# One core, two layers and a mixer in fp32: longer chains of seven-product tile pairs in the MLPs

## The chip, the cores and the metric

The kernel runs on 1 core of one Trainium2 chip. The metric is the device time of one execution in microseconds. PE is the matmul engine, PEld its weight load, DVE the vector engine, ACT the scalar engine, POOL the GpSimd engine, SP the engine whose queue issues the weight loads.

## The reference, cut to what matters

Three blocks run one after the other on 512 tokens (the first two with 16 more in front) of width 1024: a differential attention layer with its MLP, a latent attention layer with its MLP, and a mixer block (convolution and windowed attention, gated) with a third MLP; a final norm ends it. The change touches only the three MLPs, which all have this form:

```python
def conv_ffn(h, g_norm, w_in, conv_w, conv_b, w_out):
    xn = rms_norm(h, g_norm)
    a, b = jnp.split(xn @ w_in, 2, axis=-1)        # 1024 -> 2 x 2816
    ap = jnp.pad(a, ((0, 0), (CONV_W - 1, 0), (0, 0)))
    a_conv = conv_b
    for j in range(CONV_W):
        a_conv = a_conv + ap[:, j:j + L] * conv_w[j]
    return h + (jax.nn.silu(a_conv) * b) @ w_out   # 2816 -> 1024
```

## The kernel before

**Numbers.** Everything is fp32, computed on the matmul engine in three passes: an operand is split into a high part (a cast) and a low part (operand minus high part), and a product is Xh·whi + Xl·whi + Xh·wlo. So every weight that is loaded is cast once by ACT (line 162, `whi`) and subtracted once by DVE (line 170, `wlo`) or, for some chunks ("far"), by POOL (line 112).

**Tile pairs.** w_in has 22 tile pairs of 128 gate columns (a) and 128 value columns (b). A pair is computed in one of two ways. `Plain` takes two weight chunks of 512 KB and makes 96 matmuls: 2 chunks x 2 column ranges x 8 k-tiles x 3 passes, printed as line 329. `Seven` treats the pair as a 2 x 2 by 2 x 2 block product (two halves of k, two column ranges) and makes it with seven block products instead of eight, 12 matmuls each, 84 in all, printed as line 553. `p1, p6, p7, p4` accumulate one after the other in one PSUM bank A, `p5, p3` in a second, C, and `p2` has its own; between them ACT copies a running sum out of the bank (u1 after p1, bm after p5, u2 after p6, bm after p4) and DVE adds one to a product (am after p2, bm after p7, am after p3). A product that goes on in bank A has to wait for the copy or the add that reads the bank. The differences of the input columns that the seven need are made once per MLP (`differences`).

**Weights of a seven.** Its two chunks (raw_0, and raw_1 in the two buffers of tag `rawA`) are loaded together. `combine` (line 129) has POOL make four sums of 128x512, two instructions of 128x256 each: rawS, then raw_1's low half, raw_0's low half and raw_0's high half, in place. Four split chunks come of them: "a" (raw_0 as loaded, for p1 and p2), "s" (rawS and raw_0's low half, for p5 and p6), "t" (raw_1's low half and raw_0's high half, for p7 and p3), "d" (raw_1's high half, for p4; its low part is made by POOL). The buffers of the split "s" and "d" are single: the next "d" can be cast only when p4 with the last one has ended.

**Order of the work.** `plan_ffn` lists the chunks in the order of use. `get` (lines 180 to 190) issues the splits two chunks ahead of the one asked for and the loads three ahead; loads go through one queue, SP's. A load of raw_1 waits until its buffer is free, that is until POOL's split of the "d" two sevens earlier has read it. PE's order inside `turns` is as written (`in_order`); the scheduler orders the other engines, and each runs its own list in order. The 22 pairs go in four groups; after each, `group_h` multiplies the group's gated tiles by their rows of w_out (printed `po`, line 329) and adds to h. 12 of the 22 pairs are `Seven`, in twos or singly with a plain pair between their products, and 10 are `Plain`.

Of the kernel before, what the change touches and what calls it, by code (L numbers as in the profile page):

```python
# [21 lines left out]
P = 128  # L22
# [5 lines left out]
NF = 22  # L28
# [12 lines left out]
def _layout_params():  # L41
# [14 lines left out]

NPAR = _layout_params()

GROUPS = (
    (0, 6, (0, 1, 2, (3, 4, 5))),  # L60
    (6, 11, ((6, 7, 8), (9, 10))),
    (11, 17, ((11, 12, 13), (14, 15, 16))),
    (17, 22, ((17, 18, 19), (20, 21))),
)

WSPEC = [
# [13 lines left out]
class Weights:  # L80
# [8 lines left out]
    def __init__(self, net, plan, gains, raw, parts, load_ahead, split_ahead):  # L89
        self.net, self.plan, self.gains = net, plan, gains  # L90
        self.raw, self.parts = raw, parts
        self.la, self.sa = load_ahead, split_ahead
        self.nl = self.ns = self.nu = 0
        self.raws, self.split = {}, {}
        self.more, self.rows = None, []

    def load(self):
        key, aps, nk, nc_, kind = self.plan[self.nl]
# [12 lines left out]
            c = slice(c, min(c + 256, w))  # L111
            self.net.nc.gpsimd.tensor_tensor(d[:, c], a[:, c], b[:, c], op=op)  # L112

    def sources(self, n, kind, w):

        lo, hi = slice(0, 512), slice(512, 1024)
        raws = self.raws.pop(n)
        if kind == "":
            return [raws[0][:, :w]]
        if kind == "a":  # L120
            self.rows.append(raws)
            return [raws[0]]
        a = self.rows[0]
        if kind == "s":
            return [a[2], a[0][:, lo]]
        if kind == "t":
            return [a[1][:, lo], a[0][:, hi]]
        return [self.rows.pop(0)[1][:, hi]]

    def combine(self):  # L130

        lo, hi = slice(0, 512), slice(512, 1024)
        a = self.rows[-1]
        d = self.more.tile([P, 512], F32, tag="rawS", name=f"rawS{self.ns}")
        a.append(d)
        self.sums(d, a[1][:, lo], a[1][:, hi], ALU.add)
        self.sums(a[1][:, lo], a[0][:, lo], a[1][:, lo], ALU.subtract)
        self.sums(a[0][:, lo], d, a[0][:, lo], ALU.subtract)
        self.sums(a[0][:, hi], a[0][:, hi], a[0][:, lo], ALU.subtract)

    def _split(self):
        nc = self.net.nc
        n = self.ns
        key, aps, nk, nc_, kind = self.plan[n]
        w = nk * nc_
        src = self.sources(n, kind, w)
        own = kind in ("s", "d")
        pool, tag, kw = (self.more, f"w{kind}", {"bufs": 1}) if own else (self.parts, "w", {})
        wide = 512 if kind == "d" else 1024
        hi = pool.tile([P, wide], F32R, tag=tag + "hi", name=f"whi{n}", **kw)  # L150
        lo = pool.tile([P, wide], F32R, tag=tag + "lo", name=f"wlo{n}", **kw)
        h, l = hi[:, :w], lo[:, :w]
        if key[0] in self.gains:
            for k in range(nk):
                c = slice(k * nc_, (k + 1) * nc_)
                self.net.split(h[:, c], l[:, c], src[0][:, c], self.net.pc(self.gains[key[0]], k))
        else:
            far = kind == "d" or kind == "" and (n % 4 == 3 or key[0] in ("w_pair", "w_qr"))
            c0 = 0
            for r in src:  # L160
                z = r.shape[-1]
                nc.scalar.copy(h[:, c0 : c0 + z], r)  # L162
                step = z if far else (z + 1) // (1 + (z > 512))
                for a in range(0, z, step):
                    b = min(a + step, z)
                    c = slice(c0 + a, c0 + b)
                    if far:
                        self.sums(l[:, c], r[:, a:b], h[:, c].bitcast(F32), ALU.subtract)
                    else:
                        nc.vector.tensor_tensor(l[:, c], r[:, a:b], h[:, c].bitcast(F32), op=ALU.subtract)  # L170
                c0 += z
            if kind == "a":
                self.combine()
        self.split[n] = (
            h.rearrange("p (k c) -> p k c", k=nk),
            l.rearrange("p (k c) -> p k c", k=nk),
        )
        self.ns += 1
# [27 lines left out]
class Net:  # L206
# [59 lines left out]

    def plan_ffn(self, wi, wo):
        pl = []
        for k0, k1, steps in GROUPS:
            for st in steps:  # L270
                if isinstance(st, int):
                    pl += [self.chunk(wi, st), self.chunk(wi, NF + st)]
                    continue
                *fs, g = st
                a, d = [[self.chunk(wi, m + f)[1] for f in fs] for m in (0, NF)]
                u = [
                    [((wi, f, "a"), a[i] + d[i], 8, P, "a"), ((wi, f, "s"), [], 8, P, "s")]
                    + [((wi, f, "t"), [], 8, P, "t"), ((wi, f, "d"), [], 4, P, "d")]
                    for i, f in enumerate(fs)
                ]  # L280
                wa, wb = self.chunk(wi, g), self.chunk(wi, NF + g)
                if len(u) == 1:
                    pl += [*u[0][:2], wa, u[0][2], wb, u[0][3]]
                else:
                    pl += [*u[0][:2], wa, u[0][2], u[1][0], u[0][3], u[1][1], wb, *u[1][2:]]
            pl += [self.chunk(wo, m, k0, k1) for m in range(KD)]
        return pl

# [206 lines left out]
    def ffn(self, wi, wo, cw, cb, a_ranges, b_ranges, quads, ranges, nxt, gain=None):  # L495
# [8 lines left out]
        n, o = NT - t0, t0 - a0  # L504
        (s0, e0), (s1, e1) = quads
        H = e0 - s0
        with ExitStack() as cx:
# [1 line left out]
            psp = cx.enter_context(tc.tile_pool(name=self.n("pf"), bufs=6, space=PSUM, reuse_waits="tile"))  # L509
            tp = xcx.enter_context(tc.tile_pool(name=self.n("ft"), bufs=2, reuse_waits="tile"))  # L510
            R, _ = self.norm(psp, "mm", int(a0 == META))
            kmax = max(k1 - k0 for k0, k1, _ in GROUPS)
# [90 lines left out]
            class Seven:  # L603
# [6 lines left out]
                lo, hi, sl = slice(0, H), slice(e0 - a0, NT - a0), slice(e0 - s1, H)  # L610
# [48 lines left out]
                    nc.vector.tensor_tensor(me.t, me.b[:, o : o + n], me.t, op=ALU.mult)  # L659
                    self.split(*G.at(me.k, t0, NT), me.t)  # L660

            def turns(k0, *fs):

                u = [Seven(f, f - k0) for f in fs[:-1]]
                v = Plain(fs[-1], fs[-1] - k0)
                x, y = u[0], u[-1]
                x.p1(), x.p5(), v.a(0), x.p6(), x.p2(), v.a(1), x.p7()
                if x is y:
                    v.b(0), x.p3(), x.p4(), v.b(1)
                    return  # L670
                x.p3(), y.p1(), x.p4(), y.p5(), y.p6(), y.p2(), v.b(0), y.p7(), y.p3(), v.b(1), y.p4()

            def add(p, m, s, e):
                nc.vector.tensor_tensor(self.h[:, m, s:e], p, self.h[:, m, s:e], op=ALU.add)  # L674

            for k0, k1, steps in GROUPS:
                for i, st in enumerate(steps):
                    if isinstance(st, int):
                        v = Plain(st, st - k0)
                        v.a(0, 2), v.b(0, 2)  # L680
                    else:
                        with self.in_order():
                            turns(k0, *st)
                    if k0 == i == 0:
                        differences()
                if k1 < NF:
                    self.group_h(psp, wo, G, k0, k1 - k0, ranges, add)
            xcx.close()
# [1210 lines left out]
```

## Time and profile before

| | |
|---|---|
| median of 3 runs | 2097.27 us (2091.37 to 2097.52) |
| profiled execution | 2097.7 us, span 2095.9 us, mean granted clock 0.992 |
| busy share | PE 98%, PEld 90%, DVE 67%, ACT 47%, POOL 35% |
| seven pairs, plain pairs per MLP | 12, 10 |
| the third MLP in the chain of waits | 1731 to 2085 us, PE throughout |

The span runs from the first to the last instruction of the profiled execution. A busy PE says that it always had a matmul to work on, and not how fast it could be; the other engines work beside it, and matter where PE has to wait for what they make.

### The profile page before, as it was taken

Reading aid. Unit: us, or ns where it says so; the run is one execution under the profiler, and the core shown is the slowest. Engines: PE = TensorE matmul, PEld = TensorE weight load, DVE = VectorE, ACT = ScalarE, POOL = GpSimd, SP = SyncE. Lnnn points to the kernel's source line nnn. Section 1 sums busy time; section 2 is a strip of 40 time slices with the busy share of each in tenths; the row PEclk is TensorE's granted clock in tenths of the full one; section 3 lists DMA queues with packets and bytes.
Section 4 is the critical chain, followed back from the end, with each engine's and each line's share of the span. In section 5 each row is a group of like instructions: output and inputs, shape, how many; then the busy total and the mean of one; then the engine's idle time right before and its main releaser. Section 6 shows DMA issues by size and latency. Waiting matters only on the chain. (4 is left out here: it accounts for less than half of the span.)

```text
span 2095.9 us, 36290 instructions
## 1 busy us (share of the span) xinstructions
PE 2047.9 (98%) x14327; PEld 1894.5 (90%) x14327; DVE 1398.0 (67%) x2536; ACT 976.9 (47%) x1940; POOL 738.6 (35%) x837
## 2 busy tenths in 40 slices
PE   8999999999999999999999999999999999999998
PEld 7999899999999988899898998788888879899997
DVE  8787768576767576658576768675533358577674
ACT  6566545253445455445344445354432235354444
POOL 5223252344343231133345444321112244435442
PEclk9999999999999999999999999999999999999999
DMA  4121132323322211022323333222223332323322
GB/s 169 52 61 55 38 106 67 101 80 103 102 83 82 67 41 41 32 91 66 112 82 95 94 100 92 93 81 77 70 76 101 96 116 64 108 85 108 105 76 72
DMA packets 56426, 174.91 MB, mean 83 GB/s; under 512 B 6464, under 2 KB 9408, under 8 KB 56256
## 3 DMA queue, kind: packets, MB, share of 16 engines
q1 hardware_dynamic: 55824, 172.34, 26.2%
q8 instruction: 112, 1.84, 0.4%
q14 instruction: 58, 0.48, 0.1%
q10 hardware_dynamic: 432, 0.27, 0.0%
HBM read 170.45 MB, written 2.10 MB: 82 GB/s over the span
## 5 line engine op out<-in xcount | busy, mean ns | idle before, releaser
L162 ACT CAST whi<-raw 128x1024 fp32r<-128x1024 f32 (+4 forms) x460 | 382.4, 840 | 555.3 <-PE po L329 176.8
L112 POOL TENSOR_TENSOR wlo<-raw,whi 128x256 fp32r<-128x256 f32 (+1 forms) x336 | 292.1, 897 | 582.7 <-ACT whi L162 564.7
L170 DVE TENSOR_TENSOR wlo<-raw,whi 128x512 fp32r<-128x512 f32 (+2 forms) x580 | 402.8, 732 | 44.3 <-ACT whi L162 41.4
L329 PE MATMUL pf<-Xh,whi 128*128 128x256 f32 (+2 forms) x960 | 273.0, 285 | 0.0
L329 PE MATMUL pf<-Xl,whi 128*128 128x256 f32 (+2 forms) x960 | 272.4, 284 | 0.0
L329 PE MATMUL pf<-Xh,wlo 128*128 128x256 f32 (+2 forms) x960 | 272.3, 284 | 0.0
L329 PE MATMUL po<-Gl,whi 128*128 128x512 f32 (+2 forms) x709 | 238.8, 338 | 0.0
L329 PE MATMUL po<-Gh,wlo 128*128 128x512 f32 (+2 forms) x709 | 238.8, 339 | 0.0
L329 PE MATMUL po<-Gh,whi 128*128 128x512 f32 (+2 forms) x709 | 235.5, 340 | 0.0
L329 PEld LDWEIGHTS pf<-Xh,whi 128*128 128x128 f32 x960 | 183.0, 191 | 0.0
L329 PEld LDWEIGHTS pf<-Xh,wlo 128*128 128x128 f32 x960 | 183.0, 191 | 0.0
L329 PEld LDWEIGHTS pf<-Xl,whi 128*128 128x128 f32 x960 | 182.9, 191 | 0.0
L553 PE MATMUL pf<-Th,whi 128*128 128x264 f32 (+2 forms) x576 | 162.4, 282 | 0.0
L553 PE MATMUL pf<-Th,wlo 128*128 128x264 f32 (+2 forms) x576 | 162.3, 282 | 0.0
L553 PE MATMUL pf<-Tl,whi 128*128 128x264 f32 (+2 forms) x576 | 162.3, 282 | 0.0
L329 PEld LDWEIGHTS po<-Gh,wlo 128*128 128x128 f32 x709 | 133.3, 188 | 16.6
L329 PEld LDWEIGHTS po<-Gl,whi 128*128 128x128 f32 x709 | 133.4, 188 | 15.2
L329 PEld LDWEIGHTS po<-Gh,whi 128*128 128x128 f32 x709 | 132.4, 188 | 15.1
L674 DVE TENSOR_TENSOR h<-po,h 128x272 f32<-128x272 f32 (+1 forms) x96 | 53.5, 559 | 107.3 <-PE po L329 106.7
L553 PE MATMUL pf<-Xh,wlo 128*128 128x264 f32 (+2 forms) x432 | 121.9, 282 | 0.0
L553 PE MATMUL pf<-Xl,whi 128*128 128x264 f32 (+2 forms) x432 | 121.8, 282 | 0.0
L553 PE MATMUL pf<-Xh,whi 128*128 128x264 f32 (+2 forms) x432 | 121.8, 282 | 0.0
(423 smaller groups left out, 5574.4 us busy)
## 6 DMA issues: line engine op xcount, KB each, us to landing
raw<-in_w_in_dram SPq DMA_DIRECT2D x134, 512.0 KB, 3.6
raw<-in_w_up_dram SPq DMA_DIRECT2D x44, 512.0 KB, 3.3
raw<-in_w_qkv_dram SPq DMA_DIRECT2D x24, 512.0 KB, 3.6
raw<-in_w_out_dram SPq DMA_DIRECT2D x32, 384.0 KB, 3.1
raw<-in_w_out_dram SPq DMA_DIRECT2D x32, 320.0 KB, 2.9
raw<-in_w_o_dram SPq DMA_DIRECT2D x16, 512.0 KB, 3.4
raw<-in_w_dn_dram SPq DMA_DIRECT2D x16, 384.0 KB, 3.1
raw<-in_w_dn_dram SPq DMA_DIRECT2D x16, 320.0 KB, 2.9
```

What stands on the lines that cost most here:

```text
L112: self.net.nc.gpsimd.tensor_tensor(d[:, c], a[:, c], b[:, c], op=op)
L162: nc.scalar.copy(h[:, c0 : c0 + z], r)
L170: nc.vector.tensor_tensor(l[:, c], r[:, a:b], h[:, c].bitcast(F32), op=ALU.subtract)
L329: nc.tensor.matmul(ps, w, x, start=first and i == 0, stop=i == len(ops) - 1, skip_group_check=not first)
L553: nc.tensor.matmul(ps[:, :H], a, b, start=first and i == 0, stop=i == len(ops) - 1, skip_group_check=not first)
L674: nc.vector.tensor_tensor(self.h[:, m, s:e], p, self.h[:, m, s:e], op=ALU.add)
```

## The change

Of each group's pairs, all but one become `Seven`: 15 of 22 per MLP (3-4, 6-9, 11-15, 17-20), with pairs 0 to 2 plain as before and one plain pair at the end of each group. `turns` becomes `chain`: in place of a plain pair's halves, the products of the next seven stand between those of the one in front. The plan of the chunks follows that order, and `rows`, a list, becomes a dictionary, since three sevens can be in work at a time. Nothing else differs: pools, buffers, how far ahead splits and loads go, and the engines that do them are as before.

```diff
 GROUPS = (
-    (0, 6, (0, 1, 2, (3, 4, 5))),
-    (6, 11, ((6, 7, 8), (9, 10))),
-    (11, 17, ((11, 12, 13), (14, 15, 16))),
-    (17, 22, ((17, 18, 19), (20, 21))),
+    (0, 6, (0, 1, 2), (3, 4), 5),
+    (6, 11, (), (6, 7, 8, 9), 10),
+    (11, 17, (), (11, 12, 13, 14, 15), 16),
+    (17, 22, (), (17, 18, 19, 20), 21),
 )
...
         if kind == "a":
-            self.rows.append(raws)
+            self.rows[key] = raws
             return [raws[0]]
-        a = self.rows[0]
+        a = self.rows[key]
...
     def plan_ffn(self, wi, wo):
         pl = []
-        for k0, k1, steps in GROUPS:
...
-                if len(u) == 1:
-                    pl += [*u[0][:2], wa, u[0][2], wb, u[0][3]]
-                else:
-                    pl += [*u[0][:2], wa, u[0][2], u[1][0], u[0][3], u[1][1], wb, *u[1][2:]]
+        for k0, k1, front, sevens, g in GROUPS:
+            pl += [self.chunk(wi, f + z) for f in front for z in (0, NF)]
+            units = [
+                [((wi, f, "a"), [self.chunk(wi, m)[1][0] for m in (f, NF + f)], 8, P, "a")]
+                + [((wi, f, c), [], 4 if c == "d" else 8, P, c) for c in "std"]
+                for f in sevens
+            ]
+            pl += units[0][:2]
+            for x, y in zip(units, units[1:]):
+                pl += [y[0], x[2], y[1], x[3]]
+            pl += [self.chunk(wi, g), *units[-1][2:], self.chunk(wi, NF + g)]
             pl += [self.chunk(wo, m, k0, k1) for m in range(KD)]
...
-            def turns(k0, *fs):
-
-                u = [Seven(f, f - k0) for f in fs[:-1]]
-                v = Plain(fs[-1], fs[-1] - k0)
-                x, y = u[0], u[-1]
-                x.p1(), x.p5(), v.a(0), x.p6(), x.p2(), v.a(1), x.p7()
-                if x is y:
-                    v.b(0), x.p3(), x.p4(), v.b(1)
-                    return
-                x.p3(), y.p1(), x.p4(), y.p5(), y.p6(), y.p2(), v.b(0), y.p7(), y.p3(), v.b(1), y.p4()
+            def chain(k0, fs, g):
+
+                u = [Seven(f, f - k0) for f in fs]
+                v = Plain(g, g - k0)
+                x = u[0]
+                x.p1(), x.p5(), x.p6(), x.p2()
+                for y in u[1:]:
+                    y.p1(), x.p7(), x.p3(), y.p5(), x.p4(), y.p6(), y.p2()
+                    x = y
+                v.a(0), x.p7(), x.p3(), v.a(1), x.p4(), v.b(0), v.b(1)
```

The first place is POOL's list in the third MLP, in the first pair of sevens of the group 11 to 16 and behind it. A number behind raw, whi or wlo is the chunk's place in the plan; in the kernel before, sevens 11 and 12 have the "a" chunks 378 and 382, and their "d" chunks are 383 and 387; 388 and 392 are sevens 14 and 15.

```order
L112 TENSOR_TENSOR rawS388_21218<-raw388_1_21185 128x256 x2
L112 TENSOR_TENSOR raw382_0_20926<-rawS382_20950,raw382_0_20926 128x256 x2
L112 TENSOR_TENSOR raw388_1_21185<-raw388_0_21183,raw388_1_21185 128x256 x2
L112 TENSOR_TENSOR raw382_0_20926<-raw382_0_20926 128x256 x2
L112 TENSOR_TENSOR raw388_0_21183<-rawS388_21218,raw388_0_21183 128x256 x2
L112 TENSOR_TENSOR raw388_0_21183<-raw388_0_21183 128x256
L112 TENSOR_TENSOR wlo387_21179<-raw382_1_20928,whi387_21178 128x256 x2
L112 TENSOR_TENSOR raw388_0_21183<-raw388_0_21183 128x256
L112 TENSOR_TENSOR rawS392_21366<-raw392_1_21344 128x256 x2
```

In the changed kernel the chain's sevens 11 to 15 have the "a" chunks 392, 394, 398, 402 and 406, and the "d" chunks 397, 401, 405, 409 and 412. The same list there:

```order
L113 TENSOR_TENSOR wlo401_21233<-raw394_1_20967,whi401_21232 128x256 x2
L113 TENSOR_TENSOR rawS402_21279<-raw402_1_21239 128x256 x2
L113 TENSOR_TENSOR raw402_1_21239<-raw402_0_21237,raw402_1_21239 128x256 x2
L113 TENSOR_TENSOR raw402_0_21237<-rawS402_21279,raw402_0_21237 128x256 x2
L113 TENSOR_TENSOR raw402_0_21237<-raw402_0_21237 128x256 x2
L113 TENSOR_TENSOR wlo405_21376<-raw398_1_21096,whi405_21375 128x256 x2
L113 TENSOR_TENSOR rawS406_21422<-raw406_1_21382 128x256 x2
L113 TENSOR_TENSOR raw406_1_21382<-raw406_0_21380,raw406_1_21382 128x256 x2
L113 TENSOR_TENSOR raw406_0_21380<-rawS406_21422,raw406_0_21380 128x256 x2
L113 TENSOR_TENSOR raw406_0_21380<-raw406_0_21380 128x256 x2
L113 TENSOR_TENSOR wlo409_21519<-raw402_1_21239,whi409_21518 128x256 x2
```

Before, one "d" of this piece stood among the sums; now two instructions of a "d" and eight of sums alternate strictly, with nothing else between, and raw402_1, which the sums read, takes the buffer that the "d" above them (wlo401, of raw394_1) frees.

The second place is ACT's list about the copy u2 (of bank A after p6), which p7 waits for. In the kernel before, chunk 393 is the "d" of seven 14, 394 the "s" of seven 15, u2_2065 the u2 of seven 14:

```order
L162 CAST whi393_21462<-raw388_1_21185 128x512
L658 COPY bm_2052_21147<-pf_2049_21092 128x256
L565 ACTIVATE ct_2057_21254<-ct_2057_21254 128x512
L623 COPY u1_2061_21334<-pf_2060_21321 128x256
L630 COPY bm_2063_21359<-pf_2062_21346 128x256
L426 CAST Gh_1929_18933<-ct_2057_21254 128x512
L162 CAST whi394_21500<-rawS392_21366 128x512
L162 CAST whi394_21500<-raw392_0_21342 128x512
L635 COPY u2_2065_21413<-pf_2060_21321 128x256
```

In the changed kernel, chunk 405 is the "d" of seven 13, 404 the "s" of seven 14, u2_2072 the u2 of seven 13:

```order
L162 CAST whi405_21375<-raw398_1_21096 128x512
L652 COPY bm_2063_21158<-pf_2059_21074 128x256
L162 CAST whi404_21354<-rawS402_21279 128x512
L162 CAST whi404_21354<-raw402_0_21237 128x512
L629 COPY u2_2072_21337<-pf_2067_21217 128x256
L559 ACTIVATE ct_2069_21268<-ct_2069_21268 128x512
```

In both lists u2 of one seven stands behind the two casts of the next one's "s", and so behind three of the four sums that POOL makes for the next one; u1 and bm of the same seven, which stood between the "d" and the "s", now come earlier, and the next "d" and the next "s" stand side by side.

## Rows read from the trace of the kernel before

**Rows 1.** The page's busy time of each engine, share of the span and instructions

```profile
PE 2047.9 (98%) x14327; PEld 1894.5 (90%) x14327; DVE 1398.0 (67%) x2536; ACT 976.9 (47%) x1940; POOL 738.6 (35%) x837
```

**Rows 2.** PE's waits: who waited for whom, us, times, longest

```profile
PE st L391 <- POOL nr L378: 12.7, 3, 4.7
```

**Rows 3.** The chain of waits, third MLP: start us, us, what

```profile
1728.03 2.26 POOL raw L112 x2
1730.29 0.99 POOL nr L378
...
1731.32 2.08 PE st L391 x8
...
1774.76 9.89 PE pf L553 x84
1784.65 2.83 PE pf L329 x24
...
2056.52 28.11 PE po L329 x135
```

**Rows 4.** Stretches: us; busy of PE, PEld, DVE, ACT, POOL (instructions); PE clock, DMA

```profile
357.15:367.30 10.15, 10.15 (x86) 10.15 (x85) 8.99 (x15) 7.00 (x13) 2.25 (x2) 1.00 0.47 123
1058.58:1068.67 10.09, 10.09 (x87) 10.09 (x85) 9.29 (x14) 6.99 (x13) 5.67 (x6) 1.00 0.33 106
...
1908.40:1939.50 31.10, 31.10 (x267) 31.10 (x266) 25.06 (x38) 16.37 (x27) 16.68 (x18) 1.00 0.30 99
```

**Rows 5.** POOL in time, 1908 to 1956: start, us, what, count [idle before]

```profile
1911.92 1.43 POOL L112 TENSOR_TENSOR raw<-rawS,raw 128x256 f32<-128x256 f32 x2
...
1925.04 2.21 POOL L112 TENSOR_TENSOR raw<-rawS,raw 128x256 f32<-128x256 f32 x2 [8.90 <-DVE wlo L170]
...
1928.36 2.34 POOL L112 TENSOR_TENSOR wlo<-raw,whi 128x256 fp32r<-128x256 f32 x2
1930.66 1.19 POOL L112 TENSOR_TENSOR raw<-raw 128x256 f32<-128x256 f32 x1
1933.95 2.00 POOL L112 TENSOR_TENSOR rawS<-raw 128x256 f32<-128x256 f32 x2 [2.11 <-DMA raw<-in_w_up_dram]
1935.91 1.89 POOL L112 TENSOR_TENSOR raw<-raw,raw 128x256 f32<-128x256 f32 x2
1941.21 3.56 POOL L112 TENSOR_TENSOR wlo<-raw,whi 128x256 fp32r<-128x256 f32 x2 [3.40 <-ACT whi L162]
...
1948.49 1.88 POOL L112 TENSOR_TENSOR rawS<-raw 128x256 f32<-128x256 f32 x2
1950.33 3.73 POOL L112 TENSOR_TENSOR wlo<-raw,whi 128x256 fp32r<-128x256 f32 x4
```

**Rows 6.** SP in time, 1930 to 1931

```profile
1930.72 0.33 SPq L103 DMA_DIRECT2D raw<-in_w_up_dram  x1
```

**Rows 7.** ACT in time, 1908 to 1917

```profile
1915.43 0.62 ACT L162 CAST whi<-rawS 128x512 fp32r<-128x512 f32 x1 [3.75 <-PE pf L553]
...
1916.47 0.36 ACT L635 COPY u<-pf 128x256 f32<-128x256 f32 x1
```

**Rows 8.** DVE in time, 1917 to 1931

```profile
1917.92 1.29 DVE L170 TENSOR_TENSOR wlo<-raw,whi 128x512 fp32r<-128x512 f32 x2 [0.22 <-ACT whi L162]
...
1928.87 1.23 DVE L170 TENSOR_TENSOR wlo<-rawS,whi 128x512 fp32r<-128x512 f32 x1
1930.02 1.23 DVE L170 TENSOR_TENSOR wlo<-raw,whi 128x512 fp32r<-128x512 f32 x1
```

**Rows 9.** DVE's groups of one shape, 1908.4 to 1970.6: count, busy, mean ns, idle

```profile
L170 DVE TENSOR_TENSOR wlo<-raw,whi 128x512 fp32r<-128x512 f32 x20 | 15.5, 804 | 1.8 <-ACT whi L162 1.5
...
L427 DVE TENSOR_TENSOR Gl<-ct,Gh 128x512 fp32r<-128x512 f32 x4 | 3.9, 971 | 1.0 <-ACT Gh L426 1.0
...
L641 DVE TENSOR_TENSOR am<-u,pf 128x256 f32<-128x256 f32 x4 | 1.6, 410 | 0.0
```

**Rows 10.** POOL in time, at the norm ahead of the second MLP

```profile
1031.76 1.44 POOL L112 TENSOR_TENSOR raw<-raw,raw 128x256 f32<-128x256 f32 x2 [13.69 <-DMA raw<-in_w_in_dram]
```

More of the change, by code (lines that the diff above doesn't have):

```diff
@@ L94, in __init__ @@
         self.raws, self.split = {}, {}
-        self.more, self.rows = None, []
+        self.more, self.rows = None, {}
     def load(self):
@@ L112, in sums, with sources @@
             self.net.nc.gpsimd.tensor_tensor(d[:, c], a[:, c], b[:, c], op=op)
-    def sources(self, n, kind, w):
+    def sources(self, n, key, kind, w):
         lo, hi = slice(0, 512), slice(512, 1024)
@@ L127, in sources, with combine @@
             return [a[1][:, lo], a[0][:, hi]]
-        return [self.rows.pop(0)[1][:, hi]]
-    def combine(self):
+        return [self.rows.pop(key)[1][:, hi]]
+    def combine(self, a):
         lo, hi = slice(0, 512), slice(512, 1024)
-        a = self.rows[-1]
         d = self.more.tile([P, 512], F32, tag="rawS", name=f"rawS{self.ns}")
@@ L145, in _split @@
         w = nk * nc_
-        src = self.sources(n, kind, w)
+        src = self.sources(n, key[:2], kind, w)
         own = kind in ("s", "d")
@@ L172, in _split @@
             if kind == "a":
-                self.combine()
+                self.combine(self.rows[key[:2]])
         self.split[n] = (
@@ L268, in plan_ffn @@
         pl = []
-        for k0, k1, steps in GROUPS:
[L270 to L281, printed above, removed]
-                if len(u) == 1:
-                    pl += [*u[0][:2], wa, u[0][2], wb, u[0][3]]
-                else:
-                    pl += [*u[0][:2], wa, u[0][2], u[1][0], u[0][3], u[1][1], wb, *u[1][2:]]
+        for k0, k1, front, sevens, g in GROUPS:
[9 more added lines that the diff above has]
+            pl += [self.chunk(wi, g), *units[-1][2:], self.chunk(wi, NF + g)]
             pl += [self.chunk(wo, m, k0, k1) for m in range(KD)]
@@ L511, in ffn @@
             R, _ = self.norm(psp, "mm", int(a0 == META))
-            kmax = max(k1 - k0 for k0, k1, _ in GROUPS)
+            kmax = max(g[1] - g[0] for g in GROUPS)
             G = self.xpair(gp, "G", kmax, t0)
@@ L660, in p4 @@
                     self.split(*G.at(me.k, t0, NT), me.t)
-            def turns(k0, *fs):
-                u = [Seven(f, f - k0) for f in fs[:-1]]
-                v = Plain(fs[-1], fs[-1] - k0)
-                x, y = u[0], u[-1]
-                x.p1(), x.p5(), v.a(0), x.p6(), x.p2(), v.a(1), x.p7()
-                if x is y:
-                    v.b(0), x.p3(), x.p4(), v.b(1)
-                    return
-                x.p3(), y.p1(), x.p4(), y.p5(), y.p6(), y.p2(), v.b(0), y.p7(), y.p3(), v.b(1), y.p4()
+            def chain(k0, fs, g):
[7 more added lines that the diff above has]
+                v.a(0), x.p7(), x.p3(), v.a(1), x.p4(), v.b(0), v.b(1)
             def add(p, m, s, e):
                 nc.vector.tensor_tensor(self.h[:, m, s:e], p, self.h[:, m, s:e], op=ALU.add)
[L676 to L684, printed above, removed]
+            for k0, k1, front, sevens, g in GROUPS:
+                for f in front:
+                    v = Plain(f, f - k0)
+                    v.a(0, 2), v.b(0, 2)
+                    if f == 0:
                         differences()
+                with self.in_order():
+                    chain(k0, sevens, g)
                 if k1 < NF:
```

## The prediction, made before the changed kernel ran

> **What bounds the kernel now.** I read the page's busy shares first, then PE's waits, the chain of waits, and last single stretches of the MLPs. The reader is to see four things. PE is busy 98% of the span, DVE 67%, POOL 35% [rows 1]. Of PE's waits the longest in total is the norm ahead of an MLP, 12.7 us in three, on POOL's `nr` [rows 2]; none inside an MLP comes near it. The chain agrees: in the third MLP it runs on PE alone, from the norm at 1731.32 to the end at 2084.6 [rows 3]. So the MLPs are bound by the count of matmuls, and the other engines are just in time. How nearly just shows in one stretch of two sevens and a plain pair: DVE is busy 25.06 of 31.10 us, POOL 16.68 [rows 4].
>
> **What goes: matmuls.** A seven has 84 matmuls, a plain pair 96, at one pace: 84 take 9.89 us in the third MLP, 24 plain ones 2.83 [rows 3]. A block of 12 is then 1.413 us there, 10.15/7 = 1.45 in the first MLP and 10.09/7 = 1.441 in the second [rows 4]. Three pairs per MLP change sides: 3 x (1.45 + 1.441 + 1.413) = 12.9 us off PE. PE has no idle time there in which this could vanish, so all of it comes off unless a wait takes its place.
>
> **What comes: POOL, in a loop with the loads.** Each new seven adds ten POOL instructions (eight of sums, two for the "d") and takes far chunks of the plain kind away. What matters more is the time they have. In a chain they hang together: p4 of a seven ends, the next "d" is cast, POOL splits it (2 instructions), that frees a rawA buffer, the load of a raw_1 follows, POOL makes the sums, ACT casts "s" (two casts, the second behind the third sum), copies u2, and p7 begins. Before, the same loop had 18 blocks (p4 of the first seven of one pair to p7 of the first of the next, 25.4 us). Number the blocks of a chain from 0: p4 of its first seven is block 8, p7 of its third is block 19 and p7 of its fourth block 26. So from the end of block 8 PE leaves 10 blocks to the first deadline, 14.50, 14.41 and 14.13 us in the three MLPs, and 17 blocks to the second, 24.65, 24.50 and 24.02. The second exists only where there is a fifth seven, that is in the chain 11 to 15.
>
> What the loop needs, step by step. The load: POOL's "d" ends at 1928.36 + 2.34 = 1930.70, SP issues at 1930.72, POOL begins the sums at 1933.95 after idling for the DMA: 3.25 us [rows 5, 6]. ACT: "d" cast 0.62, one "s" cast 0.62 behind its last sum, u2 0.36 [rows 7], some 0.5 for the handoffs between engines (an estimate): 2.1. POOL: 2 + 6 = 8 instructions to the first deadline, counting three of the four sums; 2 + 8 + 2 + 6 = 18 to the second, with two loads.
>
> POOL's price per instruction decides. Alone it takes 1.39/2 = 0.70 (two in 1.43, the next beginning 1.39 later in its row) [rows 5]. Beside a two-operand DVE instruction it takes 2.34/2 = 1.17, and that DVE instruction 1.15 instead of 0.60 [rows 5, 8]. Three stretches in which POOL had work without a gap hold as many instructions as the second deadline wants: 6 from 1925.04 to 1931.85, 4 from 1933.95 to 1937.80, 8 from 1941.21 to 1950.33, in all 19.78 us for 18, 1.10 each [rows 5]. The bounds are 0.70 and 1.31 (0.70 + 0.61, one after the other). I take 1.10, since DVE in the chain is denser than there.
>
> First deadline: 8 x 1.10 + 3.25 + 2.1 = 14.15 us against 14.13 to 14.50: just met. Second: 18 x 1.10 + 6.5 + 2.1 = 28.4 against 24.65, 24.50, 24.02: late by 3.75, 3.9 and 4.4, in all +12.05 us. At 0.70 it is 21.2, no stall; at 1.31 32.2.
>
> **DVE in the chain.** Per seven DVE has 12 two-operand instructions of 0.80 to 0.97 (I take 0.83) and 3 PSUM adds of 0.41: 11.2 us [rows 9]; in a row each hides 0.09 of the next (two in 1.29 against 0.69) [rows 8], which leaves 9.9 against a seven's 9.89 on PE. At the pace of before it is just in time; if POOL is met more often (DVE's busy share goes from 0.81 towards 1) I count 0.8 us a period more, 2.4 over a chain's three. The add of p7, which p4 two blocks later has to wait for, stands behind four others since p2 (4 x 0.80, against two blocks of 2.83) and takes 0.41: slack 2.83 - 0.37 - 0.41 = 2.0. Late by 0.4 in a chain of four; six such chains, +2.4. In the chain of five, PE's wait for POOL covers it. Bounds: 0, and the 2.4 of a chain without slack, 14.4.
>
> **The norm ahead of the second MLP.** Two sums of a second seven now stand before `nr` in POOL's list, as they already do ahead of the third (2.26 us of raw directly before it in the chain [rows 3]). Two cost 1.44 [rows 10]; PE waits for `nr`, so +1.4. Bounds 0 (if the sums fit in the idle time ahead) and 2.3.
>
> **Costed at nothing.** ACT's 36 more casts: ACT is busy 47% [rows 1], and they replace plain casts of twice the size. Loads: as many and as large. The gated tile of the last pair: a plain pair ends each group, as a seven or a plain one did.
>
> **Sum** on the profiled execution of 2097.7 us (span 2095.9; the median of the runs shown, 2097.27, is 0.4 below): -12.9 + 12.05 + 2.4 + 1.4 = +2.95, so 2100.7 us. I predict 2101.
>
> **Rivals.**
> 1. *All of it is gained.* POOL holds 0.90 or less in the chain, or the scheduler's slack hides the second deadline: 18 x 0.85 + 8.6 = 23.9, inside 24.0. Then -12.9 + 1.4: 2086. For it: stretches at 0.70 exist, and POOL has 65% of the span idle. Against: they stand where DVE was idle, and in the chain it hardly is.
> 2. *POOL always meets DVE* (slower). Place: u2 and p7 in the chains of four and five. At 1.20 an instruction the second deadline takes 30.2, late by 5.55, 5.7 and 6.2 (17.45); the first 14.95, late by 0.45, 0.54 and 0.82 in two chains of four each (3.6). With the other terms -12.9 + 17.45 + 3.6 + 2.4 + 1.4 = +11.95: 2110. It decides from 1.15 on. For it: 2.34 and 2.26 for two beside DVE [rows 5, 8]; two instructions of a "d" took 3.56 where DVE worked without a gap [rows 5]. Against: the mean over the dense stretches is 1.10.
> 3. *One after the other.* If neither runs while the other does, a pair costs 0.70 + 0.61 = 1.31: second deadline 32.2, late by 7.55, 7.7, 8.2 (23.4), first 15.8, late by 1.3, 1.4, 1.7 (8.9): -12.9 + 23.4 + 8.9 + 2.4 + 1.4 = +23.2: 2121. Against: beside each other both were done in 1.15 to 1.17 [rows 5, 8], a little less than 1.31. The Trainium skill ("SBUF — State Buffer", section "Who interferes with whom") says that VectorE and GpSimd share a port pair under an exclusive lock, and that a VectorE instruction with two SBUF inputs contends with a GpSimd one that reads SBUF; by that rule this rival is the whole truth. The trace agrees that both slow down, and only nearly in its size.
>
> **How the numbers follow.** About 0.3% (6 us) is what a measurement here tells from no change. The forecast's mechanism has 0.40, mostly within that bound (0.33), else slower (0.05) or faster (0.02). Rival 1 has 0.28, of which 0.26 faster. Rival 2 0.22, of which 0.20 slower. Rival 3 0.10, all slower. So faster 0.28, same 0.37, slower 0.35. The range takes rival 1 in and reaches past rival 2 half way to 3: 2086 to 2117; the forecast's own range is 2094 to 2107.
>
> **What would show it.** Right: PE waits in the chain of five, at p7 of its fourth seven, for ACT's copy u2, whose "s" cast waited for POOL's sum; about 4 us each, once per MLP; sevens at 9.9 us apart from that; POOL's instructions in the chains near 1.10. Rival 1: no PE wait in the MLPs. Rivals 2 and 3: waits at p7 of the third seven in the chains of four too, and POOL's instructions at 1.2 or more. Wrong altogether: PE waiting for DVE's low parts, or at the ends of the groups, or matmuls in the chains that are slower than before.

## The result and the profile after

The changed kernel takes 2114.76 us (median of 6 runs, 2111.03 to 2120.64) against 2097.39 us for the kernel before (6 runs): 1.0093 times as long, 95% interval 1.0072 to 1.0114. The profiled execution has a span of 2112.0 us, 16.1 more than before. The line numbers of the MLP are 6 lower than before (L553 is now L547).

The page's busy time, which answers to [rows 1]:

```profile
PE 2043.7 (97%) x14219; PEld 1886.2 (89%) x14219; DVE 1467.5 (69%) x2567; ACT 1003.4 (48%) x2012; POOL 826.6 (39%) x919
```

PE has 108 matmuls fewer and is less busy, in a longer span. So PE waits. Its waits, which answer to [rows 2] (us in total, times, longest):

```profile
PE st L385 <- POOL nr L372: 12.0, 3, 4.7
PE pf L547 <- ACT u L629: 8.8, 3, 3.0
PE pf L547 <- DVE bm L641: 6.3, 10, 0.9
...
PE pf L547 <- ACT u L617: 4.9, 3, 2.6
```

Before, none of the three lower ones was there. They are, in order: p7 of the fourth seven in the chains of five, waiting for the copy u2 (L629); p4, waiting for the add of p7 (L641); p6 of the first seven in the MLPs' first groups, waiting for the copy u1 (L617).

The loop that the prediction spoke of can be read off POOL's list in the third MLP's chain of five, which answers to [rows 5] (start, us, what, count, idle before and what ended it):

```profile
1933.62 1.68 POOL L113 TENSOR_TENSOR wlo<-raw,whi 128x256 fp32r<-128x256 f32 x2 [3.79 <-ACT whi L162]
1939.08 1.89 POOL L113 TENSOR_TENSOR rawS<-raw 128x256 f32<-128x256 f32 x2 [3.78 <-DMA raw<-in_w_up_dram]
1940.93 2.34 POOL L113 TENSOR_TENSOR raw<-raw,raw 128x256 f32<-128x256 f32 x2
1943.23 2.33 POOL L113 TENSOR_TENSOR raw<-rawS,raw 128x256 f32<-128x256 f32 x2
1945.53 2.33 POOL L113 TENSOR_TENSOR raw<-raw 128x256 f32<-128x256 f32 x2
1947.82 2.33 POOL L113 TENSOR_TENSOR wlo<-raw,whi 128x256 fp32r<-128x256 f32 x2
1953.64 2.01 POOL L113 TENSOR_TENSOR rawS<-raw 128x256 f32<-128x256 f32 x2 [3.48 <-DMA raw<-in_w_up_dram]
1955.61 2.33 POOL L113 TENSOR_TENSOR raw<-raw,raw 128x256 f32<-128x256 f32 x2
1957.90 2.30 POOL L113 TENSOR_TENSOR raw<-rawS,raw 128x256 f32<-128x256 f32 x2
```

"d" of the second seven, the wait for the load, four sums, "d" of the third, the wait for the next load, three sums. ACT beside it, at its end:

```profile
1955.68 0.62 ACT L162 CAST whi<-rawS 128x512 fp32r<-128x512 f32 x1
1960.23 0.62 ACT L162 CAST whi<-raw 128x512 fp32r<-128x512 f32 x1 [3.93 <-POOL raw L113]
1960.75 0.36 ACT L629 COPY u<-pf 128x256 f32<-128x256 f32 x1
```

The second cast of "s" waits 3.93 us for POOL's third sum, u2 stands behind it, and PE starts p7 when u2 is done:

```profile
1961.17 0.39 PE L547 MATMUL pf<-Th,whi 128*128 128x256 f32 x1 [2.95 <-ACT u L629]
1961.39 0.28 PE L547 MATMUL pf<-Tl,whi 128*128 128x256 f32 x1
...
1962.21 0.41 PE L547 MATMUL pf<-Th,whi 128*128 128x256 f32 x1
1962.42 0.41 PE L547 MATMUL pf<-Tl,whi 128*128 128x256 f32 x1
```

Behind the wait the second matmul begins 0.22 after the first, the next ones 0.12 apart, and from 1962 on they begin 0.21 apart. The view by stretch says why (columns as in [rows 4]; the last but two is the granted clock):

```profile
1920.12:1986.83 66.71, 62.83 (x517) 62.42 (x516) 58.93 (x82) 37.34 (x67) 41.93 (x41) 0.97 0.34 104
1958.00:1961.10 3.10, 0.22 (x2) 0.01 (x1) 1.84 (x3) 0.87 (x3) 3.10 (x4) 1.00 0.21 84
1962.00:1965.10 3.10, 3.10 (x16) 3.10 (x16) 3.10 (x6) 1.01 (x4) 1.86 (x2) 0.50 0.11 15
...
536.40:539.80 3.40, 3.40 (x28) 3.40 (x29) 3.40 (x5) 1.76 (x4) 2.66 (x3) 1.00 0.02 5
```

The clock went to its lower level (0.50, that is 1.2 of 2.4 GHz) behind this wait. It also did so behind the same wait in the second MLP and behind the u1 wait of the third; behind the same wait in the first MLP (2.83 us) it stayed at 1.00, the last row. So a wait of 3 us here costs its 3 us, and sometimes some 1.5 to 2.5 more (16 to 26 matmuls at 0.21 instead of 0.12).

A stage runs from the first matmul of a group's pairs to the first of its projection (`po`); in the first group of an MLP it begins behind the norm's own matmuls (`st`), so that PE's wait for the norm is not in it. The twelve stages of the three MLPs take (us, one profiled execution of each kernel):

| group of pairs | before, MLP 1, 2, 3 | after | difference |
|---|---|---|---|
| 0 to 5 (two sevens before and after) | 62.11, 62.26, 61.33 | 63.51, 63.87, 64.38 | +6.1 |
| 6 to 10 (chain of four) | 53.93, 53.15, 52.29 | 53.32, 52.62, 52.04 | -1.4 |
| 11 to 16 (chain of five) | 64.11, 63.26, 62.18 | 67.16, 68.67, 66.71 | +13.0 |
| 17 to 21 (chain of four) | 53.93, 53.15, 52.30 | 53.44, 52.62, 52.05 | -1.3 |
| sum | 694.0 | 710.4 | +16.4 |

The chains of four gain a third of what their matmuls gave (1.41 to 1.45 each). The rest of the program is where it was.

### The profile page after: what moved, and what is told of

It is laid out like the page before. It is cut to its first block, busy times and chain, and to the rows that moved or that the text cites. A ratio compares the mean times of both kernels' runs of the same rounds, so it can differ in the third digit from the quotient of the medians.

```text
span 2112.0 us, 36450 instructions
## 1 busy us (share of the span) xinstructions
PE 2043.7 (97%) x14219; PEld 1886.2 (89%) x14219; DVE 1467.5 (69%) x2567; ACT 1003.4 (48%) x2012; POOL 826.6 (39%) x919
## 4 chain that ended last, share of the span: by engine, by line
PE 74%; DVE 14%; ACT 4%; POOL 4%; issue 3%; DMA 1%; SPq 0%; ACTq 0%; POOLq 0%; DVEq 0%
PE po L323 22%; PE pf L547 15%; PE pf L323 8%; PE pc L323 5%; DVE wlo L170 4%; PE pg L323 4%; PE pq L323 4%; PE pyc L323 2%; PE s L712 2%; PE pm L323 2%; PE o L1352 1%; PE pd L323 1%; ACT whi L162 1%; PE pya L323 1%; POOL raw L113 1%
## 5 line engine op out<-in xcount | busy, mean ns | idle before, releaser
L162 ACT CAST whi<-raw 128x1024 fp32r<-128x1024 f32 (+3 forms) x487 | 393.8, 819 | 546.3 <-PE po L323 194.8
L170 DVE TENSOR_TENSOR wlo<-raw,whi 128x512 fp32r<-128x512 f32 (+2 forms) x593 | 449.3, 793 | 55.5 <-ACT whi L162 53.8
L547 PE MATMUL pf<-Th,whi 128*128 128x264 f32 (+2 forms) x720 | 205.9, 286 | 20.0 <-ACT u L629 8.8
L547 PE MATMUL pf<-Tl,whi 128*128 128x264 f32 (+2 forms) x720 | 204.5, 284 | 0.0
L547 PE MATMUL pf<-Th,wlo 128*128 128x264 f32 (+2 forms) x720 | 204.3, 284 | 0.0
L323 PE MATMUL pf<-Xh,whi 128*128 128x256 f32 (+2 forms) x672 | 191.2, 285 | 0.0
L323 PE MATMUL pf<-Xl,whi 128*128 128x256 f32 (+2 forms) x672 | 190.7, 284 | 0.0
L323 PE MATMUL pf<-Xh,wlo 128*128 128x256 f32 (+2 forms) x672 | 190.5, 284 | 0.0
L547 PEld LDWEIGHTS pf<-Th,whi 128*128 128x128 f32 x720 | 136.7, 190 | 23.3 <-ACT u L629 9.4
L547 PE MATMUL pf<-Xl,whi 128*128 128x264 f32 (+2 forms) x540 | 153.7, 285 | 0.0
L547 PE MATMUL pf<-Xh,whi 128*128 128x264 f32 (+2 forms) x540 | 153.6, 285 | 0.0
L547 PE MATMUL pf<-Xh,wlo 128*128 128x264 f32 (+2 forms) x540 | 153.6, 284 | 0.0
L113 POOL TENSOR_TENSOR rawS<-raw 128x256 f32<-128x256 f32 x90 | 84.0, 954 | 152.3 <-DMA raw<-in_w_in_dram 87.0
L547 PEld LDWEIGHTS pf<-Tl,whi 128*128 128x128 f32 x720 | 137.0, 190 | 0.0
L547 PEld LDWEIGHTS pf<-Th,wlo 128*128 128x128 f32 x720 | 136.8, 190 | 0.0
```

The source lines that it names most:

```text
L323: nc.tensor.matmul(ps, w, x, start=first and i == 0, stop=i == len(ops) - 1, skip_group_check=not first)
L547: nc.tensor.matmul(ps[:, :H], a, b, start=first and i == 0, stop=i == len(ops) - 1, skip_group_check=not first)
```

## The experiments

Each was timed against the kernel before in the same runs. "Stages" is the sum above: 694.0 before, 710.4 after. "Waits for bm" are p4's waits for the add of p7, "waits for u1" those of p6, "waits for u2" those of p7.

**Is it the loop through the rawA buffers?** raw_1 gets a tile for each half, the high half with three buffers, so that the next load does not wait for POOL's "d". In exchange rawS has one buffer instead of two:

```diff
-            pool, tag = (self.more, "rawA") if i else (self.raw, "raw")
-            t = pool.tile([P, 1024], F32, tag=tag, name=f"raw{self.nl}_{i}")
+            if i:
+                for c, tag, z in ((0, "rawL", 2), (512, "rawD", 3)):
+                    t = self.more.tile([P, 512], F32, tag=tag, name=f"{tag}{self.nl}", bufs=z)
+                    self.net.nc.sync.dma_start(t, ap[:, c : c + 512])
...
-        d = self.more.tile([P, 512], F32, tag="rawS", name=f"rawS{self.ns}")
+        d = self.more.tile([P, 512], F32, tag="rawS", name=f"rawS{self.ns}", bufs=1)
```

> Only raw_1's two halves get tiles of their own (low half two buffers, high half three, rawS one instead of two), so that a load no longer waits for POOL's split of the d two sevens earlier. Theory (the loop d, load, sums, casts, u2 is too long by its two loads): two loads of 3.3 to 3.8 us leave it, 27.3 us become about 20.5 against 24 to 24.65, so PE's three waits at p7 of the fourth seven (8.8 us, ACT u) go, and with them their restarts and the stretches at the lower clock behind two of them; the waits for DVE's bm (6.3) and for u1 (4.9) stay: 14 us less than the changed kernel's waits and half-clock stretches together, about 2102 us. Rival (POOL and DVE have simply too much work in the chain): the sums come as late as before, PE's waits for u2 stay at 2 to 3 us each, 2112 to 2116.

Measured: 2120.08 us, ratio 1.0117 (1.0099 to 1.0135), stages 724.4. PE's waits in the MLPs:

```profile
PE pf L552 <- DVE bm L646: 21.3, 18, 2.5
PE pf L552 <- ACT u L622: 10.6, 3, 4.2
```

The waits for u2 are gone to the last, as the theory of the loop had it; but the other two grew from 11.2 to 31.9 us. The stages are 14 us longer, of which the time shows about 5 (the intervals of the two ratios overlap): the wait for the norm, which is not in the stages, fell from 12.0 to 4.1 us. DVE and POOL in the third MLP's last chain of four show what stands ahead of the add (first DVE, then POOL):

```profile
2047.08 1.22 DVE L175 TENSOR_TENSOR wlo<-rawL,whi 128x512 fp32r<-128x512 f32 x1
2048.22 1.22 DVE L658 TENSOR_TENSOR ct<-bm,ct 128x512 f32<-128x512 f32 x1
2049.37 1.22 DVE L175 TENSOR_TENSOR wlo<-raw,whi 128x512 fp32r<-128x512 f32 x1
2050.51 0.41 DVE L646 TENSOR_TENSOR bm<-pf,bm 128x256 f32<-128x256 f32 x1
...
2059.52 0.68 DVE L175 TENSOR_TENSOR wlo<-rawL,whi 128x512 fp32r<-128x512 f32 x1
```

```profile
2045.49 2.27 POOL L118 TENSOR_TENSOR rawS<-rawL,rawD 128x256 f32<-128x256 f32 x2 [0.63 <-DVE wlo L175]
2047.71 2.32 POOL L118 TENSOR_TENSOR rawL<-raw,rawL 128x256 f32<-128x256 f32 x2
...
2054.57 2.33 POOL L118 TENSOR_TENSOR wlo<-rawD,whi 128x256 fp32r<-128x256 f32 x2
```

While POOL works (to 2056.9), DVE and POOL go in step, one of each every 1.15 us; when POOL is idle, the same DVE instruction takes 0.68, and the next begins 0.60 after it. The add that p4 waits for is L646, behind a row of three at 1.15. In the changed kernel POOL waited for a load up to 2039.10 in this chain and left DVE alone for that time.

The run doesn't show that POOL meets DVE more often in sum. With one buffer for rawS, POOL now waits for DVE to have read the last one:

```profile
POOL rawS L118 <- DVE wlo L175: 88.1, 30, 9.6
```

In the stages of the chains of four and five POOL is busy 59% of the time (58% in the changed kernel), and DVE's 638 low-part subtractions take 494.8 us in the whole program (493.4). So the waits moved to another product; how much of that comes from the single buffer of rawS was not tried.

**Is it POOL's work?** Two of the four sums of every seven are left out (raw_1's and raw_0's low halves stay as loaded):

```diff
-        self.sums(a[1][:, lo], a[0][:, lo], a[1][:, lo], ALU.subtract)
-        self.sums(a[0][:, lo], d, a[0][:, lo], ALU.subtract)
```

> The changed kernel with two of POOL's four sums per seven left out (raw_1's low half and raw_0's low half stay as loaded), nothing else. Theory now (POOL's sums cost twice: they are late themselves, and each that meets DVE makes a DVE instruction take 1.15 instead of 0.60, so the add that p4 waits for comes late): with 6 instead of 10 POOL instructions a seven the waits for u2 and for bm both go (15.1 us), the u1 waits of the first groups (4.9) shrink by half or more, DVE's low-part subtraction of 128x512 falls from its mean of 0.79 to below 0.70: 2085 to 2092. Rival (DVE alone has too much to do in a chain, POOL does not matter to it): u2's waits go, bm's stay at 6 us or grow as they did with more d buffers: 2100 to 2110.

Measured: 2082.55 us, ratio 0.9943 (0.9926 to 0.9961), stages 682.1. What is left of PE's waits in the MLPs:

```profile
PE pf L545 <- ACT u L615: 0.4, 1, 0.4
PE pf L545 <- DVE bm L639: 0.2, 1, 0.2
```

All three kinds of wait go together, and the stages are 11.9 us shorter than before the change. Of this the chains of four have 8.3 (8.6 was costed), the chains of five 2.8 (4.3; p4 of their fourth seven still begins some 0.2 to 0.4 us late), and the first groups, with as many matmuls as before, the rest. So the matmuls are worth nearly what they were costed at. DVE has the same instructions as in the changed kernel, yet its waits went too. Its low-part subtraction of 128x512 (count, busy, mean ns), in the changed kernel and in this one:

```profile
L170 DVE TENSOR_TENSOR wlo<-raw,whi 128x512 fp32r<-128x512 f32 x449 | 369.5, 856 | 52.9 <-ACT whi L162 51.2
```

```profile
L168 DVE TENSOR_TENSOR wlo<-raw,whi 128x512 fp32r<-128x512 f32 x449 | 326.8, 760 | 55.4 <-ACT whi L160 53.6
```

It fell from 0.86 to 0.76. The 0.79 of the expectation is the mean of this line over all its shapes, and that fell to 0.715, not below 0.70; it was enough. The run doesn't say how much each engine's share in this is: it makes the loop shorter and POOL meet DVE less at the same time.

**The start of a chain.** The first seven runs p1, p5, p2, p6:

```diff
-                x.p1(), x.p5(), x.p6(), x.p2()
+                x.p1(), x.p5(), x.p2(), x.p6()
```

> Only the first seven of each chain runs p1, p5, p2, p6 instead of p1, p5, p6, p2. Theory (p6 has one block instead of three for the copy u1, which stands on ACT behind the gate of the last plain pair): the waits for u1 (0.54, 1.76, 2.62 us, one in each MLP's first group) fall by one block of 1.4 each, to about 0, 0.3 and 1.2, 3.4 us less, and the half-clock stretch behind the longest goes (1.7): about 2110. Rival (ACT is late as such at that place): the wait comes at p2's add or at p7 instead, no change, 2113 to 2117.

Measured: 2114.51 us, ratio 1.0084 (1.0066 to 1.0102), stages 708.3; the first groups' stages 62.45, 63.16 and 61.47, 4.7 us less than after and 1.4 more than before.

```profile
PE pf L547 <- ACT u L629: 9.8, 5, 3.3
PE pf L547 <- DVE bm L641: 5.9, 9, 1.0
PE pf L547 <- ACT u L617: 0.4, 1, 0.4
```

The time is that of the rival (2113 to 2117), but the u1 waits went as the theory had it: p6 had one block for the copy. In the third MLP of the changed kernel ACT's list held u1 behind the gated tile of the last plain pair (L420):

```profile
1775.63 0.62 ACT L420 CAST Gh<-ct 128x512 fp32r<-128x512 f32 x1 [0.68 <-DVE ct L593]
1776.16 0.36 ACT L617 COPY u<-pf 128x256 f32<-128x256 f32 x1
```

The time as a whole did not move: the chains took 2.6 us more in sum, and the rest of the program 3.8 more in this execution. Outside the stages single executions take 1401 to 1406 us in the kernels here (1395 and 1397 in the two with halves of raw_1, whose wait for the norm is 8 us shorter), so a gain of 2 us in the stages is not told by the total.

**The loop's start.** p4 one block later in each period:

```diff
-                    y.p1(), x.p7(), x.p3(), y.p5(), x.p4(), y.p6(), y.p2()
+                    y.p1(), x.p7(), x.p3(), y.p5(), y.p6(), x.p4(), y.p2()
```

> Only x.p4 is moved one block back in each period (y.p5, y.p6, x.p4, y.p2). Theory (p4 waits for the add of p7 because it has two blocks for it; the loop starts at p4's end): the ten waits for bm (6.3 us) go, but the loop starts a block later, so the three waits at p7 of the fourth seven grow by 1.41 to 1.45 each to about 4.3 (+4.3), and the chains of four, which met their deadline by about 0.5 us, get waits for u2 of about 1 us each (six, +6): together 4 us slower, about 2119. Rival (the wait for bm shows that DVE has too much work): DVE's waits turn up elsewhere (bm again, or low parts), and u2's waits stay near 3 us: 2113 to 2116.

Measured: 2146.65 us, ratio 1.0253 (1.0225 to 1.0281), stages 742.5.

```profile
PE pf L547 <- ACT bm L652: 37.0, 12, 4.1
PE pf L547 <- ACT u L617: 4.8, 3, 2.5
```

The waits for the add of p7 went, as expected. The wait behind the loop grew to 4 us in the chains of five (3.99 in the third MLP, 4.3 expected) and came to the chains of four (2.35 in that MLP), as expected in kind; but it landed elsewhere: on ACT p4's copy bm now stands behind the "s" casts that wait for POOL, and the next p1 needs p4's bank. I had not listed that wait; it is twelve times 3.1 us, and the kernel is 28 us slower than I wrote.

**The three edits together.**

> The three edits together (halves of raw_1 with three buffers for the high half, p2 before p6 in the first seven, p4 a block later). Theory (the gain of 12.9 us in matmuls is there and was covered by these three waits, 20 us, with their restarts and lower clock): all waits inside the MLPs below 1.5 us in sum, 2085 to 2089 against 2097.4 before, ratio 0.994 to 0.996. Rival (POOL and DVE have too much work): the waits move to other products, 2100 or more.

Measured: 2133.64 us, ratio 1.0178 (1.0161 to 1.0196), stages 737.5. It missed: some 39 us of waits are left in the MLPs. The third edit's new wait rules (31.9 us in 18 waits for bm out of ACT), and the waits for u1, which p2 before p6 alone had taken away, are back at 6.3. The rival's forecast came (2100 or more, the waits at other products), but since the third edit brings a wait of its own, the run does not tell the two theories apart.

**The clock behind a wait.** 24 matmuls, read by nothing, fill the place of the wait in the chains of five:

```diff
-                    y.p1(), x.p7(), x.p3(), y.p5(), x.p4(), y.p6(), y.p2()
+                    y.p1()
+                    if y.f == 15:
+                        for _ in range(2):
+                            block(bank(), y.wa, 0, (0, 0))
+                    x.p7(), x.p3(), y.p5(), x.p4(), y.p6(), y.p2()
```

> The changed kernel with 24 matmuls more, read by nothing, ahead of p7 of the fourth seven in each chain of five (2.83 to 2.9 us each, 8.6 in all), where PE waited 2.83, 3.00 and 2.95 us. Theory (part of the loss is the lower clock behind a PE wait, seen behind two of those three): the added matmuls take the place of the waits, the waits fall below 0.3 each, no stretch at the lower clock follows them, and the time is that of the changed kernel less 1 to 4 us: 2110 to 2114. Rival (the clock falls for another reason at these places): half-speed stretches still follow, 2115 or more.

Measured: 2112.92 us, ratio 1.0091 (1.0073 to 1.0109), stages 710.4. The third MLP's chain of five, and PE's waits:

```profile
1920.00:1987.00 67.00, 64.81 (x540) 63.97 (x539) 60.56 (x83) 36.91 (x68) 42.27 (x41) 1.00 0.33 100
```

```profile
PE pf L547 <- DVE bm L641: 9.2, 12, 1.1
PE pf L547 <- ACT u L617: 5.1, 3, 3.3
PE pf L547 <- ACT u L629: 0.3, 2, 0.2
```

The waits for u2 are filled and the clock stays at 1.00 through the chain (0.97 over it before), which bears out that the lower clock followed the waits. In time it gave nothing that can be told (2112.92 against 2114.76, the intervals overlap), and the stages are as long as without it: the waits for bm are 2.9 us longer (9.2 against 6.3).

**Where the plain pair stands.** Fifteen sevens, the plain pair among them (first group as before the change):

```diff
...
                 x.p1(), x.p5(), x.p6(), x.p2()
-                for y in u[1:]:
-                    y.p1(), x.p7(), x.p3(), y.p5(), x.p4(), y.p6(), y.p2()
+                for i, y in enumerate(u[1:]):
+                    y.p1(), x.p7()
+                    if i == 1:
+                        v.a(0)
+                    x.p3(), y.p5()
+                    if i == 1:
+                        v.a(1)
+                    x.p4(), y.p6(), y.p2()
                     x = y
-                v.a(0), x.p7(), x.p3(), v.a(1), x.p4(), v.b(0), v.b(1)
+                x.p7(), v.b(0), x.p3(), x.p4(), v.b(1)
```

The plan of the chunks follows this order.

> Fifteen sevens per MLP as in the change, but the plain pair of a group is put among its sevens: the first group as before the change (halves of the plain pair between the products of 3 and 4), in the other groups the plain pair's gate pieces stand in the second period and its value pieces about the last seven's p7 and p4. Theory (sevens standing close are what makes POOL and DVE late; PE needs the plain pair's 4 x 2 blocks as time for them): the u2 and u1 waits go (the loop gets 21 instead of 17 blocks), bm waits halve to 3 us: -12.9 + 3 to 6: 2088 to 2093. Rival (over the whole group POOL and DVE have too much work, wherever the plain pair stands): waits of 10 us or more stay, 2100 to 2112.

Measured: 2099.76 us, ratio 1.0025 (1.0014 to 1.0036), stages 694.9.

```profile
PE pf L552 <- DVE bm L646: 7.9, 9, 2.1
PE pf L552 <- ACT bm L657: 0.4, 1, 0.4
```

15 us come back by order alone. The waits for u1 and u2 went, as expected; those for bm did not halve (6.3 to 3 us was expected), and the time lies between the theory's range and the rival's. What stays is in the chains of five (65.32, 64.40 and 66.18 against 64.11, 63.26 and 62.18 before): seven of the ten waits, and the longest.

**Fourteen sevens.** Chains of four as in the change, groups one and three as before:

> Chains only where they are of four (6-9 and 17-20, as in the change); groups one and three as before the change; 14 sevens per MLP. Theory (the stages tell it: the four-chains took 0.25 to 0.6 us less than the same groups before, each with one block of 12 fewer and one wait of about 0.9; the loss stands in the first and third groups): 694.0 of the MLPs' stages fall to 691.3, time 2094 to 2097, ratio 0.997 to 1.000. Rival (groups disturb their neighbours through loads and buffers): 2099 or more.

Measured: 2095.05 us, ratio 0.9999 (0.9989 to 1.0010), stages 690.1. The stages are shorter by 3.9 us (2.7 of it in the chains of four, the rest in the first groups, which are as before), the time is not to be told from before. With the plain pair spread among the four:

> Fourteen sevens as in the run before (pairs of sevens in the first and third groups, four in the second and fourth), with the plain pair of the second and fourth groups put among its four sevens. Theory (what stands between sevens decides, four sevens can be covered): the six waits for bm (3.9 us) fall to three of 0.5 at most, the six stages of four sevens take 0.4 to 0.5 us less each, the MLPs' stages come to 687 to 689 us against 694.0: 2090 to 2094, ratio 0.997 to 0.9985. Rival (the gain is lost elsewhere as it was with fourteen sevens, whose stages were 3.9 us shorter at the same total time): 2095 to 2097.

Measured: 2093.45 us, ratio 0.9987 (0.9978 to 0.9996), stages 689.7; PE's only waits inside the MLPs:

```profile
PE pf L553 <- DVE bm L647: 1.6, 4, 0.5
```

Of the versions that leave nothing out, this one and its variant below are faster than the kernel before, by 0.13%. It keeps six of the nine exchanges per execution (8.6 us in matmuls). Its chains of four are 4.9 us shorter than the same groups before, and 2.7 show in the time.

**A sum on DVE instead of POOL.** The fourth sum of a seven as one DVE instruction of 128x512, first on the fifteen sevens with the plain pair among them:

```diff
-        self.sums(a[0][:, hi], a[0][:, hi], a[0][:, lo], ALU.subtract)
+        self.net.nc.vector.tensor_tensor(a[0][:, hi], a[0][:, hi], a[0][:, lo], op=ALU.subtract)
```

> Fifteen sevens spread as before, with the fourth of the sums (raw_0's high half) made by DVE in one instruction of 128x512 instead of by POOL in two of 128x256. Theory (a POOL instruction that meets DVE costs DVE 0.55, so two of them cost it up to 1.1, and the sum itself costs it 0.61): the waits for bm fall from 7.9 to 3 to 6 us, 2095 to 2099. Rival (DVE simply has too many instructions in these groups, and gets one more): bm's waits grow to 12 us or more, 2103 to 2110.

Measured: 2104.00 us, ratio 1.0045 (1.0032 to 1.0057), stages 700.5, 9.6 us of waits for bm and 2.4 for copies of ACT's. The rival's time came, but not for its reason. DVE is less busy, 1433.6 us against 1453.4 in the run with the fifteen sevens spread: 0.44 less for each of the 45 sevens, near the theory's 1.1 - 0.61. What the theory left out is that DVE's list runs in order. The fourth sum reads what POOL's third has made, so DVE now stops in front of it, and all that stands behind waits too:

```profile
DVE raw L139 <- POOL raw L113: 60.3, 35, 3.4
```

```profile
1935.82 0.69 DVE L139 TENSOR_TENSOR raw<-raw 128x512 f32<-128x512 f32 x1 [2.93 <-POOL raw L113]
```

That these stops are what lengthened PE's waits is argued, not shown.

> The same exchange of the fourth sum on fourteen sevens, spread. Theory: as little waiting as without it (below 1.5 us) and POOL's sums earlier, no change within 1 us of it, 2090 to 2094. Rival: DVE's extra instruction delays the adds, waits of 4 us or more, 2095 or more.

Measured: 2093.23 us, ratio 0.9987 (0.9977 to 0.9997), stages 690.8, 3.0 us of waits for bm, twice what the theory had. The time is the same as without the exchange, as it had it: here 64.4 us of such stops on DVE cost nothing that the time shows.

## Why the prediction was right or wrong

The time lies in the range (2086 to 2117) but 14 us above the value, outside the forecast's own range (2094 to 2107), and on the slower side, not "the same". That it lies in the range is luck: the upper end was set for rivals 2 and 3, and their signs, waits for u2 in the chains of four and POOL at 1.2 an instruction, did not come. By its steps:

- **Matmuls, -12.9.** Right, or nearly: 11.1 us show in the chains where two sums are left out, with some short waits remaining.
- **The loop, +12.05.** Right in mechanism, place and size: p7 of the fourth seven, once per MLP, for u2, behind the "s" cast that waited for POOL's third sum. From the end of block 8 to the start of block 26 the loop took 28.34, 28.45 and 28.17 us (28.4 forecast), 11.8 in sum beyond PE's 17 blocks. The wait at p7 itself is shorter, 2.83, 3.00 and 2.95 us, 8.8 in all, because the wait for bm at p4 (block 22) falls into the same time. In the third MLP POOL's 18 instructions took 19.3 us without the waits for loads, 1.07 each (1.10 taken), and the two loads 3.78 and 3.48 (3.25); the chains of four met their deadline. The remedy that the first experiment drew from it was wrong: taking the loads out of the loop made the kernel no faster.
- **DVE, +2.4.** Right in place (p4, for the add of p7), too small. The six chains of four waited 0.44 to 0.89 us each, 3.9 in all (0.4 each taken), and some 0.27 behind each wait (below). The chains of five waited 2.3 more, which I had counted as covered, and nearly all of it was: it is part of the loop's time. This was the term to look at: with the loop's loads out of the way it was the largest (21.3 us). I priced POOL and DVE apart, each with the other as a surcharge. Where both have work they are nearly one queue: ten POOL instructions in step with DVE took 11.4 us (2045.49 to 2056.90, above), longer than a seven's 9.89 on PE. Rivals 2 and 3 argued so, for the loop alone.
- **Costed at nothing: the chain's start.** A step that failed. The prediction's parts looked at what follows the first seven; its own p5 and p6 lost the plain pair's piece between them, so that p6 follows p1 after one block instead of three. 4.9 us in the first groups, where a plain pair's gated tile stands ahead on ACT; with p2 ahead of p6 they fell to 0.4, and the first groups took 4.7 us less.
- **The norm, +1.4.** Wrong: the two sums stand before `nr` as forecast (1.40 us), but PE's wait there was 3.33 us against 4.06. POOL's list ahead of `nr` has changed in other places too: a low part of 3 us that stood some 8 us before `nr` (939.21, `nr` at 947.40) now stands 19 us before it (929.23 and 948.42).
- **Not in the sum at all: what a wait brings with it.** The other step that failed. The waits add up to 20.0 us (0.6 where two sums are left out), but the stages are 28.3 longer than there (710.4 against 682.1). The other 9 are the matmuls about a wait. The profile counts a wait from the end of the matmul in front, 0.28 after its start, though without a wait the next begins 0.12 after it, and the second matmul behind a wait begins 0.23 instead of 0.12 after the first: 0.27 for each of sixteen waits, some 4 us. Three stretches of 16 to 26 matmuls at the lower clock cost some 5.5. Against the kernel before, the starts of the MLPs lost about 1 us less by the clock.

So of the 13 us between the forecast's +2.95 and the 16.1 of the profiled execution, the chain's start has nearly 6 and the lower clock some 5.5, DVE's term some 3 and the matmuls 2; the norm and the MLPs' starts gave 3 back (an estimate from the numbers above).

The rule that rival 3 went by agrees with the runs as far as they go. The Trainium skill ("SBUF — State Buffer", section "Who interferes with whom") names an exclusive lock on a port pair shared by VectorE and GpSimd. Here a pair in step takes 1.15 us, where the two alone take 0.60 and 0.70, so it is nearly one after the other, with a little overlap.

What stays open: whether p4 a block later would help with ACT's copy bm put ahead of the casts; how much of the waits for bm comes from POOL meeting DVE and how much from DVE's own count of instructions, since leaving out sums changes the loop and the meeting at once.

## What to carry to other kernels

When an engine on the bound gets less to do, price the engines beside it as one where they slow each other: here DVE and POOL in step, 1.15 us a pair, against the shorter time that PE leaves. Taking away the wait that shows may only move it to another product while their work stays; leaving out half of the work shows in one run whether the work is the cause. An instruction moved to another engine brings its own waits into that engine's list. And when pieces move, look at what they stood between: the same fifteen sevens cost 17 us or 4, by where the plain pair stands.

## What the runs showed of the hardware that was not expected

- POOL and DVE on two-operand instructions from SBUF go in step at 1.15 us each for as long as both have work (2045 to 2057 in the run with more buffers), DVE on 512 columns and POOL on 256; DVE's adds that read PSUM take 0.41 there as elsewhere.
- Behind waits of PE of 2.6 to 3.0 us inside otherwise full stretches the granted clock went to 0.50 in three of four cases in the changed kernel (for 16 to 26 matmuls); filled with idle matmuls, in none of three. Over the MLPs of all the traces here 0.50 followed 20 of the 32 waits between 2.1 and 3.0 us, all eight longer ones (3.3 to 4.2), and none of the 109 shorter ones (up to 1.8): the same wait of 2.5 us was followed by it or not.
